# Row slots of 1280 bytes, and the recurrence's 64x64 products laid over four quadrants of the array

## The chip, the cores and the metric

The kernel runs on one core of one Trainium2 chip. A core has TensorE (PE; its weight loads are listed as PEld), VectorE (DVE), ScalarE (ACT), GpSimd (POOL) and SyncE (SP), which issues most of the DMAs. Times are device microseconds (us) of one execution; the time of a kernel is the median of its runs. One execution of each kernel is also profiled, and the rows of the profile come from that one.

## The reference

One inference step of one layer of a hybrid decoder, for a prompt of 256 tokens and 8 single sampled tokens (T = 264 columns in all), width 2048, in fp32:

```python
x = x + 0.5 * swiglu(rmsnorm(x, n1), f1g, f1u, f1d)          # FFN1, 2048 -> 5504 -> 2048
h = rmsnorm(x, nm)
proj = h @ w_in
q, k, v = split(proj)                                        # 16 query heads, 4 kv heads of 64
o_att = sliding_window_attention(q, k, v, sinks)             # window 128
o_rwkv, shift, S = rwkv_time_mix(proj[..., ATT_COLS:], ...)  # 16 heads of 64
x = x + concat(o_att, o_rwkv) @ w_out
x = x + 0.5 * swiglu(rmsnorm(x, n2), f2g, f2u, f2d)          # FFN2
y = rmsnorm(x, final_norm)
```

The core of the time mixing is a recurrence over the tokens, for every head with a state S of 64x64:

```python
sa = einsum('bhij,bhj->bhi', S, -kk_t)
S = S * exp(lw_t)[:, :, None, :] + sa[..., None] * (kk_t * a_t)[:, :, None, :] + v_t[..., None] * k_t[:, :, None, :]
y_t = einsum('bhij,bhj->bhi', S, r_t)
```

## The kernel before

All activations lie transposed: 128 features of a row tile on the partitions, the 264 tokens in the columns. The three big parts are FFN1, the mixing (w_in, attention, recurrence, w_out) and FFN2.

**The big products.** `gemm` streams the weights in chunks of 128x512 (256 KB). SP loads a chunk (`raw`), ACT casts it to the rounded type (`hi`, L132), DVE subtracts to get the rest (`lo`, L59). Activations are split likewise into a hi and a lo row. Each 128x128 weight tile then makes three products of 264 columns, all at L75 (the helper `mm`): hi with the hi row, hi with the lo row, lo with the hi row. There are 14976 such products. In the profile they are `acc<-x,hi` and `acc<-x,lo`, where x, h, o, y or kv is the tile of the activation rows.

**The rows.** `blk` makes one tile of n slots, `ROW` floats apart, of which 264 are used; `pairs` takes the odd slot as a hi row and the even slot before it as its lo row. The rows of h (the hidden layer of an FFN) have slots of the same size in a tile of the FFN's own pool. In FFN2 that pool also holds a small tile `rt`, which stands ahead of h.

```python
t = sp.tile([P, n * ROW + (16 if tag == "y" else 0)], dt, tag=tag, bufs=1, name=uid(tag))
return [t[:, j * ROW:j * ROW + T] for j in range(n)]
```

**Side work in ticks.** After each chunk (twelve products) `gemm` calls `tick`, which moves every running generator on to its next `yield`; `pause(n)` is n ticks. A generator's instructions are so written between the chunks of the big products. A scheduler then fixes the order on each engine, near to this order.

**The recurrence** is done in chunks: 256 tokens are 4 chunks (c) of 64, and 16 heads are 8 pairs (a pair's two heads, h = 0 and 1, on the partitions 0 to 63 and 64 to 127), which go in 4 batches of 2 pairs (k). `prep` runs per pair. It makes the products of keys and queries of each chunk (`gm`), the tiles KR and BT, and near its end two sets of small products: `gv`, with the V rows that lie in `uv` (two quadrants of the array off the diagonal), and `dps`, with the states of the sampled tokens (`XD`, on the diagonal quadrants). `chain` runs per batch, when the pairs are prepared:

- DVE solves a triangular system of 32 rows for each half chunk (tiles `st`, `Xt`, `X`), which ends in TN and TT. Then come `pause(7)`, two small products with a copy after each, and a tick.
- `wus`: TT times two slices of KR at once gives W and U in one product of 64x64 by 128 columns, into one bank for each pair. ACT and DVE copy W (L622) and U (L626, into `uv`). A tick.
- `pbs`: W times BT, and W times gm (the two heads on the two diagonal quadrants); PT is copied from the first, KR takes the second in a sum.
- pN and pY: uv times BT and gm, with all 128 rows.
- three steps of the state, c = 1 to 3, a tick apart: PT times S, then S times KR into pY, then two sums on DVE.
- Ys is copied from pY on ACT; then a group norm on the way to w_out. The last batch also transposes XD (five products, L701) and copies them to XR (L703, L704), which the sampled tokens' state update reads in FFN2.

w_out takes its rows in three passes: the pairs of batches 0 and 1, those of batches 2 and 3, the attention's.

Of the kernel before, what the change touches and what calls it, by code (L numbers as in the profile page):

```python
# [30 lines left out]
ROW = 288  # L31
# [4 lines left out]
PW = (2, 1, 3, 2, 9)  # L36
ALPHA = math.exp(-0.5)
# [10 lines left out]
def body(tc, I, O):  # L48
# [47 lines left out]
    def pause(n):  # L96
        for _ in range(n):
            yield

    with ExitStack() as ctx:  # L100
# [21 lines left out]
        def mp():  # L122
            return pp.tile([P, 512], F32, tag="m", bufs=NM, name=uid("m"))
# [233 lines left out]
        def mixing_body(mx, n2, n3, XD, XR):  # L357
# [68 lines left out]
            def prep(p, bt, k, xrr, xk, xv):  # L426
# [126 lines left out]
            def chain(bt):  # L553
# [35 lines left out]
                yield from pause(7)  # L589
# [20 lines left out]
                yield  # L610
# [3 lines left out]
                wus = [mp() for _ in range(n)]  # L614
                for k in range(n):
                    for c in range(4):
                        for h in range(2):
                            r = HALF[h]
                            mm(wus[k][r, c * P:c * P + P], TT[r, k * 4 + c, :], bt.KR[k][r, 0:3:2, c, :])
                for k in range(n):  # L620
                    v = wus[k].rearrange("p (c t) -> p c t", c=4)
                    (A.copy, V.tensor_copy)[k % 2](W[:, k], v[:, 1:4, 0:64])  # L622
                for k in range(n):
                    v = wus[k].rearrange("p (c t) -> p c t", c=4)
                    for h in range(2):
                        (V.tensor_copy, A.copy)[h](uv[HALF[h], :, k, HALF[h]], v[HALF[h], :, 64:128])  # L626
                yield
                pbs = [mp() for _ in range(n)]
                for k in range(n):
                    for c in range(1, 4):  # L630
                        x = (c - 1) * P
                        for h in range(2):
                            r = HALF[h]
                            mm(pbs[k][r, x:x + 64], W[r, k, c - 1, :], bt.BT[k][r, c, r])
                        for h in range(2):
                            r = HALF[h]
                            mm(pbs[k][r, x + 64:x + P], W[r, k, c - 1, :], bt.Gm[k][h][r, c, 64:128])
                for k in range(n):
                    v = pbs[k][:, :384].rearrange("p (c t) -> p c t", c=3)
                    A.copy(PT[:, k], v[:, :, 0:64])  # L640
                    tt(V, bt.KR[k][:, 1, 1:4, :], v[:, :, 64:128], bt.KR[k][:, 1, 1:4, :], ALU.add)
# [7 lines left out]
                for k in range(n):  # L649
                    for c in range(4):  # L650
                        x = (k * 4 + c) * 64
                        for h in range(2):
                            r = HALF[h]
                            mm(pY[r, x:x + 64], uv[:, c, k, r], bt.Gm[k][h][:, c, 64:128],
                               k + c == 0, c == 0, skip_group_check=True)
# [4 lines left out]
                for c in range(1, 4):  # L660
                    ps = mp()
                    for k in range(n):
                        for h in range(2):
                            r = HALF[h]
                            mm(ps[r, k * 64:k * 64 + 64], PT[r, k, c - 1, :], S[r, k])
                    for k in range(n):
                        for h in range(2):
                            r = HALF[h]
                            x = (k * 4 + c) * 64
                            mm(pY[r, x:x + 64], S[r, k], bt.KR[k][r, 1, c, :], False, True, skip_group_check=True)  # L670
# [26 lines left out]
                if len(bts) == nbat and bt is bts[-1]:  # L697
                    ps = mp()
                    xt = mp()
                    for i in range(5):  # L700
                        TE.transpose((ps, xt)[i > 3][0:64, i % 4 * P:i % 4 * P + P], XD[:, i, :, :], ident)  # L701
                    for h in range(2):
                        A.copy(XR[HALF[h], 0:4], ps[0:64].rearrange("p (c t) -> p c t", c=4)[:, :, HALF[h]])  # L703
                        A.copy(XR[HALF[h], 4], xt[0:64, HALF[h]])  # L704
# [226 lines left out]
            for pi, ks in enumerate(PASS):  # L931
# [24 lines left out]
                k0 += len(ks)  # L956
            n3.to += pairs(blk("o", 8, F32R), *late, *xs4[:2])
            return xr

        def second_ffn(n3, xr, XR):  # L960
# [153 lines left out]
```

## Time and profile before

| | us |
|---|---|
| median of 3 runs (lowest, highest) | 1962.74 (1962.64, 1966.27) |
| the profiled execution | 1962.1 |
| its span | 1960.3 |
| PE busy in the span | 1944.7 (99%) |
| DVE busy | 1314.4 (67%) |
| ACT busy | 1036.9 (53%) |
| POOL busy | 264.0 (13%) |

The granted clock of TensorE was 0.998 in the mean. By stage: FFN1 lies at 0 to 757 us, the mixing with w_out at 757 to 1204, FFN2 after that. In the rows, "acc" is a bank for a big product and "m" a bank for a small one. The rows of the timeline give start, duration, engine, line, operation, output and inputs, shapes and a count. One fp32 product of two 64x64 tiles has two records in it. A matmul's duration runs over several others behind it, since they are pipelined: what one costs is read from start to start.

### The profile page before, as it was taken

Reading aid. Unit: us, or ns where it says so; the run is one execution under the profiler, and the core shown is the slowest. Engines: PE = TensorE matmul, PEld = TensorE weight load, DVE = VectorE, ACT = ScalarE, POOL = GpSimd, SP = SyncE. Lnnn points to the kernel's source line nnn. Section 1 sums busy time; section 2 is a strip of 40 time slices with the busy share of each in tenths; the row PEclk is TensorE's granted clock in tenths of the full one; section 3 lists DMA queues with packets and bytes.
Section 4 is the critical chain, followed back from the end, with each engine's and each line's share of the span. In section 5 each row is a group of like instructions: output and inputs, shape, how many; then the busy total and the mean of one; then the engine's idle time right before and its main releaser. Section 6 shows DMA issues by size and latency. Waiting matters only on the chain.

```text
span 1960.3 us, 45229 instructions
## 1 busy us (share of the span) xinstructions
PE 1944.7 (99%) x17011; PEld 1926.7 (98%) x17011; DVE 1314.4 (67%) x2591; ACT 1036.9 (53%) x2069; POOL 264.0 (13%) x382
## 2 busy tenths in 40 slices
PE   9999999999999999999999999999999999999998
PEld 9999999999999999999989999999999999999998
DVE  5865555655556567799988766866666666666665
ACT  5644444444444456666556755644444444444445
POOL 0401001010010122232210000210101001010012
PEclk9999999999999999999999999999999999999999
DMA  7666666656656567555556455566666666666664
GB/s 241 179 195 193 188 193 194 187 187 179 189 180 187 184 198 226 165 168 147 140 143 176 139 155 183 176 185 187 191 188 196 184 191 190 190 194 183 192 180 148
DMA packets 218875, 357.26 MB, mean 182 GB/s; under 512 B 33552, under 2 KB 72352, under 8 KB 218656
## 3 DMA queue, kind: packets, MB, share of 16 engines
q1 hardware_dynamic: 212144, 345.76, 58.9%
q10 hardware_dynamic: 6512, 8.61, 1.4%
q8 instruction: 133, 2.18, 0.4%
q14 instruction: 86, 0.70, 0.1%
HBM read 346.67 MB, written 9.69 MB: 182 GB/s over the span
## 4 chain that ended last, share of the span: by engine, by line
PE 96%; DVE 2%; issue 1%; DMA 1%; ACT 0%; SPq 0%; DVEq 0%; ACTq 0%
PE acc L75 87%; PE m L75 8%; DVE lo L59 0%; DVE Xt L59 0%; DVE st L59 0%; ACT t L69 0%; DMA x<-in_x 0%; DMA raw<-in_win 0%; DVE y L59 0%; PE m L516 0%; SPq L564 0%; DMA Xt<-sa 0%; PE m L782 0%; PE m L474 0%; DVE t L442 0%
## 5 line engine op out<-in xcount | busy, mean ns | idle before, releaser
L59 DVE TENSOR_TENSOR lo<-raw,hi 128x512 fp32r<-128x512 f32 (+1 forms) x1288 | 875.2, 683 | 513.7 <-ACT hi L132 490.7
L132 ACT CAST hi<-raw 128x512 fp32r<-128x512 f32 (+1 forms) x1288 | 777.6, 607 | 826.0 <-PE acc L75 751.7
L75 PE MATMUL acc<-x,hi 128*128 128x264 f32 x5034 | 932.3, 285 | 1.6 <-DVE o L62 1.3
L75 PEld LDWEIGHTS acc<-x,hi 128*128 128x128 f32 x5034 | 772.4, 188 | 5.2 <-ACT hi L132 1.8
L75 PE MATMUL acc<-x,lo 128*128 128x264 f32 x2517 | 708.0, 282 | 0.4 <-DVE lo L59 0.3
L75 PE MATMUL acc<-h,hi 128*128 128x264 f32 x2752 | 498.1, 284 | 0.0
L75 PEld LDWEIGHTS acc<-x,lo 128*128 128x128 f32 x2517 | 473.0, 188 | 2.6 <-DVE lo L59 1.0
L75 PEld LDWEIGHTS acc<-h,hi 128*128 128x128 f32 x2752 | 420.3, 188 | 0.0
L75 PE MATMUL acc<-h,lo 128*128 128x264 f32 x1376 | 382.6, 280 | 0.0
L75 PEld LDWEIGHTS acc<-h,lo 128*128 128x128 f32 x1376 | 258.0, 188 | 0.0
L59 POOL TENSOR_TENSOR t<-t,t 128x264 f32<-128x264 f32 x74 | 80.0, 1081 | 1099.8 <-DVE t L59 796.1
L75 PE MATMUL acc<-y,hi 128*128 128x264 f32 x648 | 122.9, 284 | 0.0
L75 PE MATMUL acc<-o,hi 128*128 128x264 f32 x648 | 120.5, 283 | 0.0
L75 PE MATMUL acc<-kv,hi 128*128 128x264 f32 x582 | 109.5, 283 | 0.0
L75 PEld LDWEIGHTS acc<-y,hi 128*128 128x128 f32 x648 | 100.3, 188 | 0.1
L75 PEld LDWEIGHTS acc<-o,hi 128*128 128x128 f32 x648 | 99.3, 188 | 0.0
L62 DVE SCALAR_TENSOR_TENSOR x<-acc,x 128x264 f32<-128x264 f32 x192 | 81.1, 427 | 25.1 <-PE acc L75 24.3
L75 PE MATMUL acc<-y,lo 128*128 128x264 f32 x324 | 90.8, 280 | 0.0
L75 PE MATMUL acc<-o,lo 128*128 128x264 f32 x324 | 90.7, 280 | 0.0
L59 DVE TENSOR_TENSOR t<-acc,t 128x264 f32<-128x264 f32 x156 | 67.4, 432 | 32.7 <-PE acc L75 32.7
L75 PEld LDWEIGHTS acc<-kv,hi 128*128 128x128 f32 x582 | 89.2, 188 | 0.0
L75 PE MATMUL acc<-kv,lo 128*128 128x264 f32 x291 | 81.5, 280 | 0.0
(280 smaller groups left out, 1533.9 us busy)
## 6 DMA issues: line engine op xcount, KB each, us to landing
raw<-in_gu SPq DMA_DIRECT2D x688, 256.0 KB, 3.4
raw<-in_dn SPq DMA_DIRECT2D x224, 256.0 KB, 2.8
raw<-in_win SPq DMA_DIRECT2D x152, 256.0 KB, 3.4
raw<-in_dn SPq DMA_DIRECT2D x160, 192.0 KB, 2.7
raw<-in_wout SPq DMA_DIRECT2D x64, 256.0 KB, 3.4
xsp<-x ACTq DMA_DIRECT2D x16, 132.0 KB, 3.1
x<-xsp SPq DMA_DIRECT2D x16, 132.0 KB, 4.1
ld<-in_sT SPq DMA_DIRECT2D x16, 128.0 KB, 3.4
```

The lines of the kernel that those rows point to most:

```text
L59: return e.tensor_tensor(out=out, in0=a, in1=b, op=op)
L62: return V.scalar_tensor_tensor(out=out, in0=a, scalar=s, in1=b, op0=op0, op1=op1)
L75: return TE.matmul(out, lhsT, rhs, start=start, stop=stop, **k)
L132: A.copy(hi[:, :w], raw[:, :w])
```

## The change

- `ROW` goes from 288 to 320 floats: slots of 1280 bytes for every tile of rows. `rt` in FFN2 goes from 16 to 48 floats.
- `gv` and `dps` are written alternately, so that products of diagonal and of off-diagonal quadrants follow each other.
- W and U are separate products of 64x64: U goes to the other half of the partitions (`ub`), W stays (`wb`) and is left out for chunk 0, where nothing reads it. That makes 28 products of 64 columns where 16 of 128 were, in each batch. W is copied by one ACT instruction, U by one on DVE and one on ACT.
- `pbs` becomes `pb` (to the other half) and `gb`, alternating; PT is copied in two ACT instructions.
- In a step of the state, PT times S and S times KR alternate, since pY is now kept with its halves exchanged. Ys is copied back in four pieces, two on ACT and two on DVE.
- `pause(7)` becomes 8 ticks in batch 0; the ticks ahead of W and U, and ahead of `pb`, become two.
- The transposes of XD get a generator of their own (`turned`), three ticks later, with a tick before their copies; what still runs at the end of w_out is drained there.

```diff
-ROW = 288
+ROW = 320
+LAG = (8, 7, 7, 7)
...
-                gv = mp()
-                for c in range(4):
+                gv, dps = mp(), mp()
+                for i in range(NB):
+                    c, g = i // 2, i % 2
                     for h in range(2):
                         r, o = HALF[h], HALF[1 - h]
-                        mm(gv[r, c * 64:c * 64 + 64], bt.Gm[k][h][o, c, 0:64], bt.UV[o, c, k, r])
+                        mm(dps[r, 2 * i:2 * i + 2], st[i // 4][r, i % 4, :], XD[r, 6:8, p, i])
+                        if h == g:
+                            mm(gv[r, c * 64:c * 64 + 64], bt.Gm[k][h][o, c, 0:64], bt.UV[o, c, k, r])
                 A.copy(KR[:, 2], gv[:, :256].rearrange("p (c t) -> p c t", c=4))
-                dps = mp()
-                for i in range(NB):
-                    for h in range(2):
-                        r = HALF[h]
-                        mm(dps[r, 2 * i:2 * i + 2], st[i // 4][r, i % 4, :], XD[r, 6:8, p, i])
...
-                yield from pause(7)
+                yield from pause(LAG[bt.i])
...
-                yield
+                yield from pause(2)
...
-                wus = [mp() for _ in range(n)]
+                ub, wb = mp(), mp()
                 for k in range(n):
                     for c in range(4):
+                        x = (k * 4 + c) * 64
                         for h in range(2):
-                            r = HALF[h]
-                            mm(wus[k][r, c * P:c * P + P], TT[r, k * 4 + c, :], bt.KR[k][r, 0:3:2, c, :])
-                for k in range(n):
-                    v = wus[k].rearrange("p (c t) -> p c t", c=4)
-                    (A.copy, V.tensor_copy)[k % 2](W[:, k], v[:, 1:4, 0:64])
-                for k in range(n):
-                    v = wus[k].rearrange("p (c t) -> p c t", c=4)
-                    for h in range(2):
-                        (V.tensor_copy, A.copy)[h](uv[HALF[h], :, k, HALF[h]], v[HALF[h], :, 64:128])
-                yield
-                pbs = [mp() for _ in range(n)]
+                            r, o = HALF[h], HALF[1 - h]
+                            mm(ub[o, x:x + 64], TT[r, k * 4 + c, :], bt.KR[k][r, 2, c, :])
+                            if c:
+                                mm(wb[r, x:x + 64], TT[r, k * 4 + c, :], bt.KR[k][r, 0, c, :])
+                v = wb[:, :n * 256].rearrange("p (k c t) -> p k c t", k=n, c=4)
+                A.copy(W, v[:, :, 1:4, :])
+                v = ub[:, :n * 256].rearrange("p (k c t) -> p c k t", k=n, c=4)
+                for h in range(2):
+                    (V.tensor_copy, A.copy)[h](uv[HALF[h], :, :, HALF[h]], v[HALF[1 - h]])
+                yield from pause(2)
+                pb, gb = mp(), mp()
                 for k in range(n):
                     for c in range(1, 4):
-                        x = (c - 1) * P
+                        x = (k * 3 + c - 1) * 64
                         for h in range(2):
-                            r = HALF[h]
-                            mm(pbs[k][r, x:x + 64], W[r, k, c - 1, :], bt.BT[k][r, c, r])
-                        for h in range(2):
-                            r = HALF[h]
-                            mm(pbs[k][r, x + 64:x + P], W[r, k, c - 1, :], bt.Gm[k][h][r, c, 64:128])
+                            r, o = HALF[h], HALF[1 - h]
+                            mm(pb[o, x:x + 64], W[r, k, c - 1, :], bt.BT[k][r, c, r])
+                            mm(gb[r, x:x + 64], W[r, k, c - 1, :], bt.Gm[k][h][r, c, 64:128])
...
                         for h in range(2):
-                            r = HALF[h]
+                            r, o = HALF[h], HALF[1 - h]
                             mm(ps[r, k * 64:k * 64 + 64], PT[r, k, c - 1, :], S[r, k])
-                    for k in range(n):
-                        for h in range(2):
-                            r = HALF[h]
-                            x = (k * 4 + c) * 64
-                            mm(pY[r, x:x + 64], S[r, k], bt.KR[k][r, 1, c, :], False, True, skip_group_check=True)
+                            mm(pY[o, x:x + 64], S[r, k], bt.KR[k][r, 1, c, :], False, True, skip_group_check=True)
...
-                    A.copy(Ys[k][:, :NP], pY[:, k * NP:(k + 1) * NP])
+                    for h in range(2):
+                        (A.copy, V.tensor_copy)[h](Ys[k][HALF[h], :NP], pY[HALF[1 - h], k * NP:(k + 1) * NP])
...
-                rt = fp.tile([88, 16], F32, name="rt")
+                rt = fp.tile([88, 48], F32, name="rt")
```

What the change does to the order of PE's instructions is shown at two stretches of batch 1 and one of the preparation. A row has its number, its line, the operation, output and inputs with the tiles' numbers, the shape, and how often it follows itself. `acc` rows are big products, `kr,TT` the W and U products, `BT,W` and `gm,W` those of `pbs` or `pb` and `gb`.

PE before, batch 1, around the W and U products:

```order
5246 L75 MATMUL acc_13959<-x_107,lo_14007 128x264
5247 L75 MATMUL acc_13959<-x_108,hi_14036 128x264 x2
5248 L75 MATMUL acc_13959<-x_108,lo_14037 128x264
5249 L75 MATMUL acc_13959<-x_108,hi_14036 128x264
5250 L75 MATMUL m_13583<-kr_11703,TT_12420 64x128 x8
5251 L75 MATMUL m_13584<-kr_12069,TT_12420 64x128 x8
5252 L75 MATMUL acc_13959<-x_108,hi_14036 128x264
5253 L75 MATMUL acc_13959<-x_108,lo_14037 128x264
5254 L75 MATMUL acc_13959<-x_108,hi_14036 128x264 x2
```

The same place after the change:

```order
5346 L76 MATMUL acc_13963<-x_109,lo_14100 128x264
5347 L76 MATMUL acc_13963<-x_109,hi_14099 128x264 x2
5348 L76 MATMUL m_13625<-kr_11703,TT_12420 64x64
5349 L76 MATMUL m_13626<-kr_11703,TT_12420 64x64
5350 L76 MATMUL m_13625<-kr_11703,TT_12420 64x64 x3
5351 L76 MATMUL m_13626<-kr_11703,TT_12420 64x64
5352 L76 MATMUL m_13625<-kr_11703,TT_12420 64x64
5353 L76 MATMUL m_13626<-kr_11703,TT_12420 64x64
5354 L76 MATMUL m_13625<-kr_11703,TT_12420 64x64
5355 L76 MATMUL m_13626<-kr_11703,TT_12420 64x64
5356 L76 MATMUL m_13625<-kr_11703,TT_12420 64x64
5357 L76 MATMUL m_13626<-kr_11703,TT_12420 64x64
```

Two rows of eight 128-column products are now a run of single 64-column products that alternate between U's bank (the lower number) and W's; the second pair's follow in the same manner.

PE before, batch 1, from the W and U products to the first reader of W:

```order
5251 L75 MATMUL m_13584<-kr_12069,TT_12420 64x128 x8
5252 L75 MATMUL acc_13959<-x_108,hi_14036 128x264
5253 L75 MATMUL acc_13959<-x_108,lo_14037 128x264
5254 L75 MATMUL acc_13959<-x_108,hi_14036 128x264 x2
5255 L75 MATMUL acc_13959<-x_108,lo_14037 128x264
5256 L75 MATMUL acc_13959<-x_108,hi_14036 128x264 x2
5257 L75 MATMUL acc_13959<-x_108,lo_14037 128x264
5258 L75 MATMUL acc_13959<-x_109,hi_14077 128x264 x2
5259 L75 MATMUL acc_13959<-x_109,lo_14078 128x264
5260 L75 MATMUL acc_13959<-x_109,hi_14077 128x264
5261 L75 MATMUL m_13638<-BT_12288,W_13184 64x64 x2
5262 L75 MATMUL m_13638<-gm_12206,W_13184 64x64
```

After the change, the last of the large products ahead of that reader, and the reader:

```order
5380 L76 MATMUL acc_14138<-x_106,hi_14140 128x264 x2
5381 L76 MATMUL acc_14138<-x_106,lo_14141 128x264
5382 L76 MATMUL acc_14138<-x_107,hi_14194 128x264 x2
5383 L76 MATMUL acc_14138<-x_107,lo_14195 128x264
5384 L76 MATMUL acc_14138<-x_107,hi_14194 128x264 x2
5385 L76 MATMUL acc_14138<-x_107,lo_14195 128x264
5386 L76 MATMUL acc_14138<-x_107,hi_14194 128x264 x2
5387 L76 MATMUL acc_14138<-x_107,lo_14195 128x264
5388 L76 MATMUL m_13714<-BT_12288,W_13195 64x64
5389 L76 MATMUL m_13715<-gm_12206,W_13195 64x64
5390 L76 MATMUL m_13714<-BT_12288,W_13195 64x64
5391 L76 MATMUL m_13715<-gm_12242,W_13195 64x64
```

Before, 12 large products stand between the last W product and the first product that reads W; after the change 22 do (with two transposes of a pair being prepared among them), and BT,W and gm,W alternate one by one, where two of the one and two of the other went together.

PE before, preparation of a pair, `gv` (uv,gm) and `dps` (XD):

```order
5170 L75 MATMUL m_13367<-uv_11876,gm_13247 64x64
5171 L75 MATMUL m_13367<-uv_11876,gm_13283 64x64
5172 L75 MATMUL m_13367<-uv_11876,gm_13247 64x64
5173 L75 MATMUL m_13367<-uv_11876,gm_13283 64x64
5174 L75 MATMUL m_13367<-uv_11876,gm_13247 64x64
5175 L75 MATMUL m_13367<-uv_11876,gm_13283 64x64
5176 L75 MATMUL m_13367<-uv_11876,gm_13247 64x64
5177 L75 MATMUL m_13367<-uv_11876,gm_13283 64x64
5178 L75 MATMUL m_13377<-XD,ld_13287 64x2 x8
5179 L75 MATMUL m_13377<-XD,ld_13289 64x2 x8
```

After the change, the same pair:

```order
5253 L76 MATMUL m_13379<-XD,ld_13298 64x2
5254 L76 MATMUL m_13378<-uv_11876,gm_13258 64x64
5255 L76 MATMUL m_13379<-XD,ld_13298 64x2 x3
5256 L76 MATMUL m_13378<-uv_11876,gm_13294 64x64
5257 L76 MATMUL m_13379<-XD,ld_13298 64x2
5258 L76 MATMUL m_13378<-uv_11876,gm_13258 64x64
5259 L76 MATMUL m_13379<-XD,ld_13298 64x2 x3
5260 L76 MATMUL m_13378<-uv_11876,gm_13294 64x64
```

The eight uv,gm products stood ahead of the sixteen XD products; each now stands between XD products.

More of the change, by code (lines that the diff above doesn't have):

```diff
@@ L638, in chain @@
+                            mm(gb[r, x:x + 64], W[r, k, c - 1, :], bt.Gm[k][h][r, c, 64:128])
+                v = pb[:, :n * 192].rearrange("p (k c t) -> p k c t", k=n, c=3)
+                for h in range(2):
+                    A.copy(PT[HALF[h]], v[HALF[1 - h]])
+                v = gb[:, :n * 192].rearrange("p (k c t) -> p k c t", k=n, c=3)
                 for k in range(n):
-                    v = pbs[k][:, :384].rearrange("p (c t) -> p c t", c=3)
-                    A.copy(PT[:, k], v[:, :, 0:64])
@@ L678, in chain @@
                 for k in range(n):
-                    A.copy(Ys[k][:, :NP], pY[:, k * NP:(k + 1) * NP])
+                    for h in range(2):
+                        (A.copy, V.tensor_copy)[h](Ys[k][HALF[h], :NP], pY[HALF[1 - h], k * NP:(k + 1) * NP])
                     A.copy(Ys[k][:, NP:T], XD[:, 7, bt.p0 + k, :])
@@ L697, in chain, with turned @@
                 if len(bts) == nbat and bt is bts[-1]:
[L698 to L704, printed above, removed]
+                    spawn(turned())
+                yield
+            def turned():
+                yield from pause(3)
+                ps, xt = mp(), mp()
+                for i in range(5):
+                    TE.transpose((ps, xt)[i > 3][0:64, i % 4 * P:i % 4 * P + P], XD[:, i, :, :], ident)
+                yield
+                for h in range(2):
+                    A.copy(XR[HALF[h], 0:4], ps[0:64].rearrange("p (c t) -> p c t", c=4)[:, :, HALF[h]])
+                    A.copy(XR[HALF[h], 4], xt[0:64, HALF[h]])
                 yield
@@ L956, in mixing_body @@
                 k0 += len(ks)
+            drain(list(tasks))
             n3.to += pairs(blk("o", 8, F32R), *late, *xs4[:2])
```

6 lines of the change are left out of this document (3 added, 3 removed).

## Prediction

> **What bounds the kernel now.** I read the page's busy shares and its chain first, then the busy times cut by stage, then the chain in order of time, and last single rows of the PE timeline.
>
> ```profile
> span 1960.3 us, 45229 instructions
> PE 1944.7 (99%) x17011; PEld 1926.7 (98%) x17011; DVE 1314.4 (67%) x2591; ACT 1036.9 (53%) x2069; POOL 264.0 (13%) x382
> PE 96%; DVE 2%; issue 1%; DMA 1%; ACT 0%; SPq 0%; DVEq 0%; ACTq 0%
> ```
> ```profile
> 0.00:66.00 66.00, 64.84 (x509) 63.93 (x510) 45.62 (x78) 38.99 (x75) 8.26 (x18) 1.00 0.67 218
> 66.00:757.00 691.00, 691.00 (x5760) 691.00 (x5760) 419.49 (x711) 344.46 (x619) 89.90 (x89) 1.00 0.63 190
> 757.00:1204.00 447.00, 441.11 (x4559) 424.64 (x4559) 361.31 (x962) 278.23 (x700) 73.94 (x177) 1.00 0.55 160
> 1204.00:1960.30 756.30, 747.70 (x6190) 747.09 (x6188) 488.02 (x842) 375.18 (x677) 91.89 (x98) 0.99 0.62 185
> ```
> ```profile
> 65.86 691.26 PE acc L75 x5760
> ...
> 1149.08 54.83 PE acc L75 x457
> ...
> 1258.34 690.05 PE acc L75 x5712
> ```
>
> The second block has, after start and end, the busy us of PE, PEld, DVE, ACT and POOL, the granted clock, the DMA share and GB/s. TensorE carries 96% of the chain, at full clock. In FFN1 (66 to 757) it never pauses: 691.26 / 5760 = 120.01 ns for each 264-column product. So only three things can move the end: how long one large product takes, how long the small products of the recurrence hold TensorE in the mixing stage (757 to 1204), and the waits there, at most 447.0 - 441.1 = 5.9 us of idle time. ACT and DVE copies count only where they make TensorE wait.
>
> **Row slots.** A slot was 288 floats, 1152 bytes, which is four and a half times 256; now it is 1280, five times 256. Before, the hi and lo rows of a pair (neighbouring slots) start half a 256-byte line apart; afterwards all start alike. The `rt` tile grows by 32 floats (128 bytes), which shifts the rows of h in FFN2 by the same half line. Does placement change a product's time? FFN1 and FFN2 run the same code on the same shapes, and their h rows differ in placement: in FFN2 the hi and lo rows have swapped half lines. The time by tile h (FFN2 first, then FFN1):
>
> ```profile
> 1290.00:1948.00 658.00, 251.39 (x2063) 1.00 0.62 186
> 66.00:757.00 691.00, 248.70 (x2064) 1.00 0.63 190
> ```
>
> Equal counts and equal clock, 2.69 us apart. The long piece of FFN2 in the chain says the same of all its products: 690.05 / 5712 = 120.81 ns, 0.80 above FFN1's; x 5712 that is 4.6 us. The w_out piece has 54.83 / 457 = 119.98, nothing to win. I take it that rows placed alike run at FFN1's 120.0, and credit 4.6, rounded to **-5 us** for some loss inside the mixing stage that no long piece shows. No row has the new placement (hi and lo alike), so the ends are the two tile rows: 120.5 (248.70 / 2064, which holds the overlap at the ends of stretches) against 121.9 (251.39 / 2063), 1.36 ns apart. All 14976 large products going the bad way would be +20 us; the good end is -6. I take the good end, since most of the program's rows are at it already.
>
> **Four quadrants.** A 64x64 product in fp32 appears as two records (16 products kr,TT as x32). Rows of batch 3's chain, and of batch 1's preparation:
>
> ```profile
> 1065.09 1.96 PE L75 MATMUL m<-kr,TT 64*64 64x128 f32 x32
> 1066.98 0.33 PE L782 MATMUL m<-C,t 128*128 128x128 f32 x1
> ...
> 1070.27 0.28 PE L75 MATMUL m<-BT,W 64*64 64x64 f32 x4
> 1070.39 0.28 PE L75 MATMUL m<-gm,W 64*64 64x64 f32 x4
> 1070.50 0.28 PE L75 MATMUL m<-BT,W 64*64 64x64 f32 x4
> ...
> 1071.79 1.28 PE L75 MATMUL m<-uv,BT 128*64 128x64 f32 x31
> 1072.85 0.22 PE L75 MATMUL m<-gm,uv 128*64 128x64 f32 x1
> ```
> ```profile
> 1079.31 0.45 PE L75 MATMUL m<-S,PT 64*64 64x64 f32 x8
> 1079.59 0.40 PE L75 MATMUL m<-kr,S 64*64 64x64 f32 x8
> 1079.92 0.28 PE L75 MATMUL m<-qb,ld 128*128 128x8 f32 x1
> ```
> ```profile
> 940.11 0.51 PE L75 MATMUL m<-uv,gm 64*64 64x64 f32 x10
> 940.40 0.22 PE L75 MATMUL m<-XD,ld 64*64 64x2 f32 x2
> 940.45 0.23 PE L75 MATMUL m<-uv,gm 64*64 64x64 f32 x2
> 940.48 0.20 PE L75 MATMUL m<-XD,ld 64*64 64x2 f32 x2
> 940.50 0.22 PE L75 MATMUL m<-uv,gm 64*64 64x64 f32 x2
> 940.54 0.20 PE L75 MATMUL m<-XD,ld 64*64 64x2 f32 x2
> 940.56 0.23 PE L75 MATMUL m<-uv,gm 64*64 64x64 f32 x2
> 940.60 0.73 PE L75 MATMUL m<-XD,ld 64*64 64x2 f32 x20
> ...
> 942.45 0.49 PE L75 MATMUL m<-tw,ld 65*128 65x264 f32 x1
> ```
>
> With two quadrants in use, eight records (four BT, four gm) start in 0.23 us: 29 ns each. At 940.11 gm alone has 10 in 0.29, the same. Between 940.40 and 940.60 the gm products (off-diagonal quadrants) and the XD products (diagonal) go together, and 12 records start in 0.20 us: 17 ns each. Four quadrants nearly double the rate; I price an alternated record at 14.5 (half of 29) to 17.
> - W and U (kr,TT): 16 products of 128 columns take 1.89 us. They become 28 of 64 columns, 56 records: 24 products in fours, 48 x 14.5 to 17 = 0.70 to 0.82, and four U products of chunk 0 in pairs, 8 x 29 = 0.23, with about 0.1 to change over: 1.03 to 1.15. Saving 0.74 to 0.86, in four batches 3.0 to 3.4.
> - BT,W and gm,W: 48 records, 1.39 at 29, become 0.70 to 0.82: 0.57 to 0.69, in four batches 2.3 to 2.8.
> - A step of the state (S,PT and kr,S): 0.61 us for 16 records, of which 16 x 29 = 0.46 is rate. 0.23 to 0.27 afterwards: 0.19 to 0.23 for each of 12 steps, 2.3 to 2.8.
> - gv with XD: 2.34 us for two pairs (32 gm records, 64 XD). XD alone runs at 0.53 / 20 = 26 ns, so 64 are 1.7, with gm under them: 1.8 with the change-over, at most 0.5 saved, less since part of it overlaps already: 1.2 to 2.0 over four.
>
> Sum 8.8 to 11; I take **-10 us**. All of it lies on the path, as TensorE is busy there.
>
> The Trainium skill ("TensorE: Matmul & The Clock Gate", Part 3, The mechanism) says that a weight load overlaps products in flight only when its row group differs. In the new order W and U of one head share rows, so by that rule nothing doubles, and this part of the sum is about 0. The trace does not bear it out: uv,BT uses all 128 rows in every product and only changes column halves, and starts at (1072.85 - 1071.79) / 31 = 34 ns, near the 29 of products that differ in rows.
>
> **Waits.** A tick is a chunk of twelve large products, 12 x 120.0 = 1.44 us. The first and second dependent steps get one tick more (batch 0 also one ahead of them), and the five transposes of XD move to a task of their own, three ticks later.
>
> ```profile
> PE m L75 <- DVE W L622: 1.4, 2, 1.1
> ...
> PE m L75 <- DVE PT L59: 1.0, 1, 1.0
> PE m L75 <- ACT TT L609: 0.7, 1, 0.7
> PE m L701 <- ACT XR L703: 0.4, 1, 0.4
> ```
> ```profile
> 1022.84 0.35 DVE L622 COPY W<-m 128x192 f32<-128x192 f32 x1
> ```
>
> In batches 1 and 2 TensorE waits for W's second copy, which stands on DVE behind the solve of a later batch; it is one ACT copy now, and by the new order 22 large products lie between W's products and their use where 12 lay: 1.2 us more, and the longest of the two waits is 1.1. I take 1.4 off. The XR wait goes too (0.4; `XR` is next read in FFN2). The waits for TN (PT, 1.0) and TT (0.7) stay: the orders show batch 0's products after TN in the same place of the stream, and as many as before behind TT in batch 1. **-2 us**; ends 0 (each moves elsewhere) and -4 (TT and the smaller ones go as well). What is late next is uv: its DVE half is now one of 64x512, behind the same solve, but uv is read behind BT,W, 0.8 us on. Each batch ends two ticks later; that is covered by the large products of the next batch, and in the last batch by w_out, whose first pass needs batches 0 and 1 only. The two Ys copies that move to DVE replace a W and a uv copy there: 0.
>
> **What takes some back.** A large product also needs its lo chunk, which DVE subtracts, and in places DVE has nothing to spare:
>
> ```profile
> 840.00:860.00 20.00, 20.00 (x163) 19.70 (x162) 19.64 (x55) 13.47 (x32) 7.43 (x14) 1.00 0.57 175
> 980.00:1000.00 20.00, 18.67 (x148) 18.15 (x148) 19.95 (x44) 12.68 (x26) 4.50 (x11) 1.00 0.52 147
> ```
>
> DVE is at 19.6 and 19.95 of 20 us, and around 990 PE idles 1.3 us. Where DVE is full, a shorter TensorE only waits longer. If a fifth of the stage is like that, a fifth of 12 us returns: **+2.5**, from 0 to +8.
>
> **Sum.** -5 - 10 - 2 + 2.5 = -14.5 on the profiled 1962.1 us (span 1960.3 and 1.8 around it): 1947.6. The median of the three runs, 1962.74, lies 0.6 above it: **1948 us**, own range 1941 to 1955. A measurement here tells about 0.2%, 4 us, from no change.
>
> **Rivals.**
> - DVE sets the pace in most of mixing, or the waits move instead of going: row slots -5, quadrants and waits -12, +11 back, about 1957; its half above 1959 is no change. For it: the two full rows. Against: DVE is busy 361 of the stage's 447 us.
> - Products that share rows don't overlap: 56 records at 29 are 1.6 us against 1.89, the rest as before; slots and waits stay: about 1955.
> - Slower: rows placed alike run like FFN2's h. At 1.36 ns on all 14976 it is +20, with -9.5 for the rest: about 1973. It decides from about 0.65 ns a product on. For it: no row shows the new placement. Against: hi and lo start unlike in both rows that differ, so neither is a sign of it.
> - Rows placed alike are faster than any seen: 1 ns is 15 us, 3 ns would give about 1905. No row speaks for it but that placement counts.
>
> **Chances.** Forecast 0.60, DVE or moved waits 0.17, no overlap 0.09, slower placement 0.09, faster placement 0.05. Faster by over 0.2%: 0.60 + 0.09 + half of 0.17 + 0.05 = 0.82; within: 0.09; slower: 0.09. The range 1937 to 1961 leaves out the two placement rivals and the tail.
>
> **What would show it.** FFN2's h time at 248.7 and its long piece at 120.0 ns a product (slots); W and U rows alternating, in 1.0 to 1.2 us a batch, and BT,gm in 0.8 (quadrants); no wait of PE for W or XR (waits); DVE near 20 of 20 with PE waiting for lo, or a new wait for uv, would be the first rival. A long piece of FFN1 off 120.0 would make the whole forecast wrong.

## The result and the profile after

Over twelve runs each, the changed kernel takes 1962.63 us (1959.22 to 1964.30) and the kernel before 1966.44 us (1962.64 to 1967.94): a ratio of 0.9984 with a 95% interval of 0.9977 to 0.9992. That is some 3 us, where 14.5 were forecast, and 1.6 us outside the range. The profiled executions are 1962.1 us before and 1962.95 us after. They do not show the gain, because the profiled run of before was a quick one: its granted clock was 0.998, and it lies 4.3 us under the median of the twelve.

The page of the changed kernel, and its mixing stage among the busy times by stage (PE, PEld, DVE, ACT, POOL, clock, DMA share, GB/s):

```profile
span 1961.2 us, 45431 instructions
PE 1937.3 (99%) x17107; PEld 1919.6 (98%) x17107; DVE 1317.8 (67%) x2591; ACT 1039.8 (53%) x2067; POOL 258.7 (13%) x382
PE 96%; DVE 2%; ACT 1%; issue 1%; DMA 0%; DVEq 0%; ACTq 0%
```
```profile
757.00:1204.00 447.00, 433.64 (x4608) 417.27 (x4607) 362.17 (x955) 278.88 (x692) 69.25 (x177) 0.98 0.55 158
```

TensorE is busy 7.5 us less in the stage's window (433.64 for 441.11), with DVE at its 362. Two columns are new: PE now idles 447.0 - 433.6 = 13.4 us there, where it was 5.9, and the granted clock is 0.98 where it was 1.00. The chain in order of time shows what the two stages make of it:

```profile
65.74 691.23 PE acc L76 x5760
...
1150.25 59.09 PE acc L76 x492
...
1263.77 685.48 PE acc L76 x5712
```

FFN1 is as before. FFN2's long piece takes 685.48 us for its 5712 products, 120.0 ns each, where it took 690.05: 4.6 us won. But it starts at 1263.77 where it started at 1258.34: **the mixing stage is 5.4 us longer**. The gain of the rows was paid back by the recurrence.

The quadrants themselves do what was forecast. In batch 2 the 56 records of W and U take 1.21 us to the next product's start, by the PE timeline:

```profile
1018.57 1.28 PE L76 MATMUL m<-kr,TT 64*64 64x64 f32 x56
1019.78 0.27 PE L734 MATMUL m<-C,dkv 128*8 128x128 f32 x1
```

Before, they took 1.89 us there. In the other three batches they now take 1.08 to 1.09, where they took 1.89 to 2.27. Counted in this way, to the start of the next product and without waits or half clock, all four parts of the quadrants can be read from the two traces. W and U saved 3.5 us over the batches, BT,W and gm,W 3.2, the twelve steps of the state 12 x (0.61 - 0.39) = 2.6, and gv with XD 1.0: together 10.3.

What took the time is in PE's waits:

```profile
PE m L76 <- DVE Xt L60: 3.4, 1, 3.4
PE acc L76 <- DVE o L63: 3.1, 1, 3.1
PE m L76 <- ACT uv L626: 1.6, 2, 1.4
```

The first is in batch 2, and DVE's timeline tells why: U's copy to uv stands behind the solve of batch 3 (st, Xt) and starts 7 us after the W and U products are done. PE has finished BT,W and gm,W long before:

```profile
1026.92 0.23 DVE L60 TENSOR_TENSOR st<-X,Xt 128x70 f32<-128x70 f32 x1
1027.18 0.69 DVE L626 COPY uv<-m 64x512 f32<-64x512 f32 x1
1027.79 0.22 DVE L60 TENSOR_TENSOR Xt<-Xt,st 128x70 f32<-128x70 f32 x1
```
```profile
1024.40 0.22 PE L76 MATMUL m<-gm,W 64*64 64x64 f32 x1
1028.02 0.30 PE L76 MATMUL m<-uv,BT 128*64 128x64 f32 x2 [3.40 <-DVE Xt L60]
```

The second long wait is near 992 us, for the attention's `o` on a full DVE. Cut into pieces of 2 us (PE busy, clock, DMA share, GB/s), it shows the other cost:

```profile
990.00:992.00 2.00, 1.08 (x9) 1.00 0.65 193
992.00:994.00 2.00, 0.00 (x0) 1.00 0.19 69
994.00:996.00 2.00, 1.86 (x10) 0.65 0.58 155
996.00:998.00 2.00, 2.00 (x11) 0.50 0.37 108
998.00:1000.00 2.00, 2.00 (x18) 1.00 0.36 82
```

PE stands still for over 3 us, and then **runs at half clock** for some 3.4: 10 or 11 products in 2 us instead of 17. There are four stretches at half clock in the stage, from 994, 1011, 1028 and 1080 us. The first three last 3.4 us each, the fourth 6.8; half of these 17.1 us, 8.5 us, is lost. The run shown of the kernel before has none in this stage. Only the first and the third stand behind a wait of over 3 us. Ahead of the second there is no wait over 0.5 us, but 3.8 us of small products; ahead of the fourth stand a wait of 0.94 us and products of 8 columns. So 5.1 of the 8.5 us are not explained by long waits.

The account of the mixing stage: 7.5 us more idle time and 8.5 us of lost clock, less what the quadrants saved, give the +5.4 that was measured. By this the quadrants saved 10.6 us, in agreement with the 10.3 read from their own rows and with the size forecast.

### The profile page after: what moved, and what is told of

Same layout as the page of the kernel before. It is cut to its first block, busy times and chain, and to the rows that moved or that the text cites. A ratio compares the mean times of both kernels' runs of the same rounds, so it can differ in the third digit from the quotient of the medians.

```text
span 1961.2 us, 45431 instructions
## 1 busy us (share of the span) xinstructions
PE 1937.3 (99%) x17107; PEld 1919.6 (98%) x17107; DVE 1317.8 (67%) x2591; ACT 1039.8 (53%) x2067; POOL 258.7 (13%) x382
## 4 chain that ended last, share of the span: by engine, by line
PE 96%; DVE 2%; ACT 1%; issue 1%; DMA 0%; DVEq 0%; ACTq 0%
PE acc L76 88%; PE m L76 7%; DVE lo L60 1%; ACT t L70 0%; DVE y L60 0%; DMA x<-in_x 0%; DVE st L60 0%; DVE Xt L60 0%; ACT hi L133 0%; DVE t L777 0%; ACT BT L522 0%; ACT L70 0%; PE m L517 0%; DMA ld<-in_sT 0%; DVE uv L626 0%
## 5 line engine op out<-in xcount | busy, mean ns | idle before, releaser
L76 PEld LDWEIGHTS acc<-x,hi 128*128 128x128 f32 x5034 | 785.4, 190 | 6.9 <-DVE o L63 3.4
L76 PE MATMUL acc<-x,lo 128*128 128x264 f32 x2517 | 721.2, 287 | 0.8 <-DVE lo L60 0.8
L76 PE MATMUL acc<-h,lo 128*128 128x264 f32 x1376 | 387.8, 284 | 0.0
```

The source lines that it names most:

```text
L76: return TE.matmul(out, lhsT, rhs, start=start, stop=stop, **k)
```

## The experiments

My theory after the result: the rows win 4.6 us; the quadrants win about 10 on TensorE; but there TensorE is at the pace of VectorE's in-order queue, so the time turns into waits, and waits over some length halve the clock behind them. The rivals: a half clock that comes from using four quadrants, not from idling; waits that only the one copy of U causes; or the added ticks as the cause. Ratios are to the kernel before on the same chip, with 95% intervals; not all kernels of a section ran on one chip.

### The rows: alone, left out, and with the old rt

```diff
-ROW = 288
+ROW = 320
...
-                rt = fp.tile([88, 16], F32, name="rt")
+                rt = fp.tile([88, 48], F32, name="rt")
```

The first kernel is the old one with these lines alone, the second the changed one without them, the third the old one with `ROW` alone.

> The kernel before, with the slots of 320 floats and the larger rt tile alone. If the row slots do what the two traces show in FFN2 (690.05 us for 5712 products before, 685.48 after), this is 4.6 us faster than before, a ratio of 0.9977, and FFN2's long piece is again at 120.0 ns a product. If the slots only moved something else in the whole change, its ratio is 1.000 and the long piece stays at 120.8.

> The changed kernel with the old slots (288 floats, rt of 16). If the slots are worth 4.6 us and the rest of the change gains about 10 on TensorE and gives it all back in the mixing stage (7.5 us of new idle time and 7.8 us of half clock), this is as fast as before within 2 us, a ratio of 0.999 to 1.001. If the rest of the change has a gain of its own that the slots spoil, it is faster than the changed kernel, under 0.997.

> The kernel before with slots of 320 floats and the old rt: in FFN2 the rows of h start half a 256-byte line away from all other rows, but hi and lo alike. If it matters that a pair's hi and lo start alike, FFN2's h products are at 120.0 ns as with the larger rt. If it matters where they start, h's products stay near the 121.9 ns of before, and FFN2's long piece is at about 686.9 to 688 us in place of 685.5.

Measured: rows alone 0.9978 (0.9968 to 0.9988); the changed kernel with old rows 1.0014 (1.0005 to 1.0023), a little above what was expected; of the third kernel, one run. FFN2's long piece with rows alone, and the third kernel's piece and h rows (FFN1, FFN2):

```profile
1259.01 685.49 PE acc L75 x5712
```
```profile
1258.82 687.65 PE acc L75 x5712
```
```profile
66.00:757.00 691.00, 248.66 (x2064) 1.00 0.64 190
1290.00:1948.00 658.00, 250.65 (x2064) 1.00 0.63 186
```

So the rows are worth what was forecast, and all of the change's gain is theirs; with the old rows, the rest of the change makes the kernel slower by 0.0014. The third kernel splits the gain: slots of 1280 bytes alone give 2.4 us of 4.6 (687.65), the shift by `rt` the other 2.2. There hi and lo of h start alike and h in FFN2 still takes 250.65 us, not 248.66 as in FFN1: where the rows start counts, not only that a pair starts alike. Only starts 128 bytes apart were compared; that placement repeats every 256 bytes, as the prediction's reasoning has it, no run shows.

### The wait for U, and idle time on purpose

The changed kernel with both copies of U on ScalarE:

```diff
-                    (V.tensor_copy, A.copy)[h](uv[HALF[h], :, :, HALF[h]], v[HALF[1 - h]])
+                    A.copy(uv[HALF[h], :, :, HALF[h]], v[HALF[1 - h]])
```

> The changed kernel with both copies of U on ScalarE, so that neither stands behind the solve on VectorE. The 3.4 us wait of batch 2 goes. If the clock's half rate behind it (1028 to 1032 us) comes from that idle time, it goes too, and the kernel is about 5 us faster than the changed one, a ratio of 0.996 to before. If the half rate has nothing to do with the wait (for instance comes from the use of four quadrants), the granted clock there stays at 0.5 and it is 3.4 us, 0.9967. If the wait only moves to the next reader, it is the changed kernel's 0.998.

Measured: 0.9987 (0.9979 to 0.9996), no gain. The wait for U is gone, and its time stands elsewhere:

```profile
PE m L76 <- DVE Xt L60: 5.0, 2, 3.0
PE acc L76 <- DVE o L63: 3.3, 1, 3.3
PE m L76 <- ACT TT L608: 2.4, 1, 2.4
```

The rows on Xt are now waits of N,PT, the next reader, behind the same solve. The wait moved, as the third of the cases expected. A new wait of 2.4 us for TT, with TensorE almost wholly idle from 1020 to 1022 us, has no half clock behind it (pieces of 2 us: PE busy, clock, DMA share, GB/s):

```profile
1020.00:1022.00 2.00, 0.02 (x2) 1.00 0.31 86
1022.00:1024.00 2.00, 1.94 (x61) 1.00 0.44 115
```

Next, waits in the kernel before, far from any small products:

```diff
...
+        def gap(k):
+            ps, pt, g = mp(), mp(), tmp()
+            for j in range(2):
+                behind(mm(ps[:, j * P:j * P + P], ones, ones))
+            A.copy(g[:, :256], ps[:, :256])
+            for _ in range(k):
+                tt(G, g[:, :256], g[:, :256], g[:, :256], ALU.add)
+            held[0] = mm(pt[:, :P], ones, g[:, :P])
...
+                    if begin and pi and o == 8:
+                        gap(pi)
```

> The kernel before, with five added waits of TensorE in FFN1, one in each of its later parts: a small product waits for a copy on ScalarE and 1, 2, 3, 4 and 5 additions on GpSimd, about 1 us each, and the next large product stands behind it. No four quadrants are used there. If idle time lowers the granted clock, the long ones (3 us and over) are followed by some 3.4 us at 0.5, which cost 1.7 us each beside the gap, and the short ones are not. If idle time is not the cause, the clock stays at 1.00 behind all five, and the time is longer by the gaps alone, about 20 us.

One run: 1992.49 us. Two of the five gaps, and the pieces of 2 us behind them (PE busy, clock, DMA share, GB/s):

```profile
248.84 0.49 PE L76 MATMUL m<-t,ones 128*128 128x128 f32 x2 [1.15 <-POOL t L60]
```
```profile
373.95 0.49 PE L76 MATMUL m<-t,ones 128*128 128x128 f32 x2 [1.84 <-POOL t L60]
```
```profile
248.00:250.00 2.00, 1.16 (x9) 1.00 0.74 214
250.00:252.00 2.00, 2.00 (x19) 1.00 0.11 35
...
374.00:376.00 2.00, 2.00 (x12) 0.71 0.28 97
376.00:378.00 2.00, 2.00 (x11) 0.50 0.00 0
378.00:380.00 2.00, 2.00 (x17) 0.94 0.47 128
```

After 1.15 us of idling the clock stays at 1.00; after 1.84 us (2.1 from start to start of the products) it falls to 0.5, and so after the three longer ones. The pieces behind the second gap lack 2 x (0.29 + 0.50 + 0.06) = 1.7 us of full clock, half of 3.4 us. So idle time alone is enough, and the rival that it takes four quadrants falls: FFN1 has no such products. The Trainium skill ("TensorE: Matmul & The Clock Gate", HAM oscillation) describes this, with gaps over some 3.4 us as the limit. The trace does not agree with the limit, as 1.84 us of idling were enough here.

The length of the gap alone does not decide, however: the 2.4 us in the kernel above were harmless. Nor does it take a gap: in this same run, with the old products, the clock falls at 1112 us (0.56 and 0.50 in the next two pieces of 1 us), and TensorE was busy all through the 3.4 us before, 1.8 us of them with products of 8 columns. Within a trace, all slow stretches start a whole number of times 3.41 us apart: in the changed kernel at 994.6, 1011.7, 1028.7 and 1079.9 us, which is 5, 5 and 15 times. That would fit a clock that is set at fixed moments by what TensorE did since the last one; this was not tested. Whether the quadrants have a part in the two stretches of the changed kernel without a long wait stays open too.

The last kernel of this section fills the wait for U with 24 idle products in batch 2:

```diff
+                for _ in range(24 if bt.i == 2 else 0):
+                    mm(pN[:, :P], ones, ones)
```

> The changed kernel with 24 products of ones (128x128, their result not used) ahead of batch 2's uv,BT, where TensorE waits 3.4 us for U. They add work and take nothing away. If idle time lowers the clock, TensorE has no gap there now, the stretch behind (1028 to 1032 us) stays at 1.00 in place of 0.5, and the kernel is 1 to 2 us faster in spite of the added work, 0.997 to 0.998. If not, the clock is 0.5 there all the same, and the time is the changed kernel's or up to 1 us more.

```profile
1024.90 5.62 PE L76 MATMUL m<-ones 128*128 128x128 f32 x48
1030.45 1.15 PE L76 MATMUL m<-uv,BT 128*64 128x64 f32 x32
```
```profile
1028.00:1030.00 2.00, 2.00 (x20) 1.00 0.14 46
1030.00:1032.00 2.00, 2.00 (x57) 1.00 0.27 67
```

The clock stays at 1.00 where it was 0.5, as expected, but the kernel is slower: 1.0017 (1.0008 to 1.0026). The 48 records took 5.5 us and so outlasted the wait by 2; and N,PT then waited 3.3 us for DVE, with half clock behind that wait instead.

### Ticks alone, quadrants alone

The first is the changed kernel with the old ticks (below; the last edit stands at both places), the second the old products with new rows and new ticks (and the moved transposes):

```diff
-LAG = (8, 7, 7, 7)
+LAG = (7, 7, 7, 7)
...
-                yield from pause(2)
+                yield
```

> The changed kernel with the ticks as before (7 for every batch, one tick ahead of W and U and ahead of pb); quadrants, rows and the moved transposes stay. If the longer spacing is what pushes the solve of one batch onto the next one's copies, the 3.4 us wait for U and the 3.3 us wait for o shrink, the clock stays up, and it is 5 to 10 us faster than the changed kernel, 0.993 to 0.996 of before. If the spacing does what it is written for, W's and PT's products wait for their copies instead, and it is as fast as the changed kernel or slower, 0.998 or more.

> The kernel before with the new rows and the new ticks (and the moved transposes), but the old products on two quadrants. Beside the kernel with the rows alone (0.9978) this tells what the ticks cost by themselves. If the ticks cause the new waits, they are here too, with half clock behind them, and it is 5 us or more slower than rows alone, 1.000 and over. If TensorE's shorter work is what uncovers VectorE, there are no waits over 2 us here and the ratio stays at 0.997 to 0.998.

Measured: quadrants without ticks 0.9981 (0.9972 to 0.9990), ticks without quadrants 0.9999 (0.9990 to 1.0007). With rows alone at 0.9978 and both at 0.9984, the ticks (with the moved transposes) cost 4 us with the old products, and with the new ones nothing that the intervals tell; the quadrants gain nothing without the ticks. With the old products the ticks bring a wait of 3.0 us for `lo` on VectorE and a slow stretch behind it, so they make waits of their own. The mixing stage of the kernel without ticks, where its FFN2 starts, and its one slow stretch there:

```profile
757.00:1204.00 447.00, 433.23 (x4649) 416.22 (x4648) 363.34 (x961) 281.96 (x697) 72.69 (x177) 1.00 0.56 160
```
```profile
1259.24 685.48 PE acc L76 x5712
```
```profile
1084.00:1086.00 2.00, 2.00 (x18) 0.92 0.64 157
1086.00:1088.00 2.00, 2.00 (x23) 0.50 0.77 254
1088.00:1090.00 2.00, 2.00 (x14) 0.73 0.35 71
```

This is the cleanest sight of the loss. PE is busy 7.8 us less than with rows alone (441.0), and FFN2 starts at 1259.24 where rows alone start it at 1259.01. The stage's clock rounds to 1.00; the slow stretch costs 1.7 us. So of some 9 us that the quadrants saved, 7.8 have become idle time and 1.7 lost clock. Of the 13.8 us that PE idles in the stage, 10.6 are waits for VectorE.

### VectorE with less to do

If VectorE's queue sets the pace, the quadrants must pay once it has room. Three kernels have the recurrence's sixteen reciprocals replaced by a quick operation:

```diff
-                V.reciprocal(b, nps[:, :T])
+                ts(V, b, nps[:, :T], 0.0, ALU.mult, 2.8e-5, ALU.add)
...
-                V.reciprocal(r, r)
+                ts(V, r, r, 0.0, ALU.mult, 0.1, ALU.add)
```

> The kernel before with the new rows alone, and with VectorE relieved: the sixteen reciprocals of the recurrence's heads (1.80 us each) are replaced by a multiply-and-add of about 0.43 us that writes a constant, so the normalisation of the keys and of the group norm is left out. That takes some 22 us off VectorE in the mixing. If TensorE is bound by its own work there, it gains little, 2 to 4 us of the 5.4 us of waits, so a ratio of 0.996 to 0.997. If VectorE sets the pace, more.

> The changed kernel with the same sixteen reciprocals left out. If VectorE hides the gain of the quadrants, then with VectorE relieved the waits of 13.4 us fall below 6, the clock stays at 0.997 or more, and it is 6 to 10 us faster than the kernel with rows alone and the same relief: a ratio of 0.990 to 0.993. If the quadrants gain nothing on TensorE's side, or the order of dependent steps makes the waits whatever VectorE has to do, it stays at the same ratio as its partner or above it.

> The changed kernel with the old ticks and the same sixteen reciprocals left out. Beside the two others this tells ticks from quadrants once VectorE has room: if the ticks are what spreads the steps far enough, it has 3 us or more of waits for W, U and PT and is slower than the changed kernel with the same relief; if they only delay, it is as fast or faster, 0.990 to 0.993.

Measured: rows alone 0.9974 (0.9963 to 0.9984), the changed kernel 0.9940 (0.9927 to 0.9954), the one without ticks 0.9944 (0.9931 to 0.9956). Rows alone hardly move (0.9978 before); with the quadrants the same relief brings 0.0044, less than was expected. The two now differ by 0.0034, 6.7 us, where they could not be told apart. The chain's FFN2 piece, rows alone and changed:

```profile
1260.45 685.48 PE acc L75 x5712
```
```profile
1254.85 685.48 PE acc L76 x5712
```

The changed one still has one wait of 6.4 us (`kr,TT` for TT's copy on ACT), so this is not yet all of the 10 us. **The gain is there, and VectorE's part of the recurrence hides it.** Ticks or none make no difference that can be told.

Can it be had with nothing left out? Three more ways were tried. One chunk's lo part in four to GpSimd, in the changed kernel:

```diff
...
-                hi, lo = ready or chunk(src[:, k0 * P:k1 * P], k1 - k0, V, ahead)
+                hi, lo = ready or chunk(src[:, k0 * P:k1 * P], k1 - k0, G if k0 == ease else V, ahead)
...
-                gemm(ps, I["win"][t], n2.xs, tick)
+                gemm(ps, I["win"][t], n2.xs, tick, ease=12)
```

> The changed kernel with the lo part of every fourth chunk of w_in subtracted on GpSimd instead of VectorE (38 of 152, some 26 us of VectorE's 362 in the mixing). If VectorE's load there is what makes TensorE wait, the idle time of 13.4 us falls below 8, the clock stays nearer to 1.00, and the kernel is 6 to 10 us faster than the changed one, 0.993 to 0.995. If the order of the dependent steps makes the waits whatever VectorE's load, it stays at 0.998; a slower GpSimd that holds up the lo chunks would show as waits for lo on POOL and a ratio above 0.998.

Slower, 1.0040 (1.0027 to 1.0053). VectorE's busy time over the span is 1319.3 us where the changed kernel has 1317.8, though some 26 us were taken off it: other operations of VectorE became longer. Of the costliest groups in the mixing, one in the changed kernel and the same with the lo parts on GpSimd:

```profile
L63 DVE SCALAR_TENSOR_TENSOR t<-pj,nmu,t 128x264 f32<-128x264 f32 x24 | 11.5, 485 | 1.2 <-ACT t L70 1.0
```
```profile
L63 DVE SCALAR_TENSOR_TENSOR t<-pj,nmu,t 128x264 f32<-128x264 f32 x24 | 15.9, 662 | 5.9 <-ACT t L70 5.7 <-ACT t L415 0.2
```

The sixteen reciprocals to GpSimd, for the same three kernels:

```diff
...
-                V.reciprocal(b, nps[:, :T])
+                A.copy(b, nps[:, :T])
+                tt(G, b, b, bc(neg, (P, T)), ALU.pow)
...
-                V.reciprocal(r, r)
+                tt(G, r, r, bc(neg, (P, T)), ALU.pow)
```

> The kernel before with the new rows, and the recurrence's sixteen reciprocals computed on GpSimd (as a power of -1, with a copy on ScalarE ahead of the eight that read a bank) instead of VectorE. Nothing is left out. If GpSimd does one in 2 us or less, this is the kernel with rows alone or a little faster, 0.997 to 0.998; if one takes many microseconds there, its steps come later and the kernel is slower than 1.000.

> The changed kernel with the same sixteen reciprocals on GpSimd. If VectorE's load is what hides the quadrants' gain, and GpSimd is quick enough, this is 4 to 8 us faster than its partner with rows alone, 0.993 to 0.995, and faster than both kernels. If the gain only showed because the normalisations were left out, it stays at 0.998.

> The changed kernel with the old ticks and the sixteen reciprocals on GpSimd. As fast as the one with the new ticks, 0.993 to 0.995, if ticks no longer matter once VectorE has room; faster than it if the added ticks only delay.

Ratios of 1.2616, 1.2735 and 1.2621: one power takes 42.5 us, which answers nothing about the quadrants. The costliest group of GpSimd in the first of them:

```profile
L59 POOL TENSOR_TENSOR t<-t,neg 128x264 f32<-128x264 f32 x16 | 679.9, 42499 | 44.9 <-ACT t L69 34.7 <-ACT t L444 10.1
```

Last, plain copies to ScalarE, for the same three; the edit of the second is shown, and the first moves the W and U copies of the old products instead:

```diff
-                    (V.tensor_copy, A.copy)[h](uv[HALF[h], :, :, HALF[h]], v[HALF[1 - h]])
+                    A.copy(uv[HALF[h], :, :, HALF[h]], v[HALF[1 - h]])
...
-                        (A.copy, V.tensor_copy)[h](Ys[k][HALF[h], :NP], pY[HALF[1 - h], k * NP:(k + 1) * NP])
+                        A.copy(Ys[k][HALF[h], :NP], pY[HALF[1 - h], k * NP:(k + 1) * NP])
...
-                    V.tensor_copy(s0, tp[:, 256:384])
+                    A.copy(s0, tp[:, 256:384])
```

> The kernel before with the new rows, and VectorE relieved by copies alone: W, U and the third of an attention tile's transposes (0.29 to 0.41 us each, 28 copies, some 9 us) go to ScalarE. Nothing is left out. With the old products TensorE has little idle time to win back: 0.996 to 0.998.

> The changed kernel with U, Ys and the same transposes' copies on ScalarE (some 10 us off VectorE, under half of what leaving out the reciprocals took). If VectorE's load hides the quadrants' gain, some of it shows: 3 to 5 us faster than the changed kernel, 0.9955 to 0.997, and as fast as its partner with rows alone or faster. If only the order of dependent steps counts, it stays at 0.998 or more, and ScalarE's queue takes VectorE's place among the waits.

> The changed kernel with the old ticks and the same copies on ScalarE. 0.9955 to 0.997 likewise if VectorE's load is what counts; if it is faster than the one with the new ticks by 2 us or more, the ticks only delay.

Measured: 1.0006 (0.9998 to 1.0015), 0.9999 (0.9990 to 1.0007) and 0.9995 (0.9986 to 1.0004): the first clearly slower than without the edit, the others no faster. VectorE is busy 10 us less in the second's stage, and TensorE idles 15.3 us there, where it idled 13.4. The waits of the second:

```profile
PE m L76 <- DVE st L60: 6.9, 2, 4.7
PE acc L76 <- DVE o L63: 3.3, 1, 3.3
```

So VectorE's busy time alone is not the measure. What the reciprocals have and the copies have not is length: 1.8 us, in a queue that runs in order. Leaving them out takes off load and also shortens the steps that the solve waits for; which of the two counts was not told apart. No kernel that computes everything beat the one with the rows alone, and that one (0.9978) is not told from the changed kernel (0.9984).

## Why the prediction was wrong, step by step

- **Row slots, -5: right.** 4.57 us in FFN2's long piece, 0.9978 for the rows alone. Its reason was half right: the third kernel of the first group has hi and lo alike and only 2.4 of the 4.6 us.
- **Four quadrants, -10: right on TensorE, wrong for the time.** The rate was sized rightly (W and U in 1.08 to 1.21 us, forecast 1.03 to 1.15; 10.3 us in all). "All of it lies on the path, as TensorE is busy there" is the sentence that failed. TensorE was 98.7% busy in that stage, but its work came at the pace at which VectorE handed it over, and a shorter TensorE waited longer.
- **Waits, -2: wrong in sign.** W's wait went from 1.4 to 0.2 us and XR's is gone, as said. But the idle time grew by 7.5 us. I named uv as what is late next and put no price on it: "0.8 us on" was set against a copy that came 7 us after its products.
- **"Each batch ends two ticks later; that is covered": wrong** with the old products, where the ticks, with the moved transposes, cost 4 us (0.9999 against 0.9978).
- **What takes some back, +2.5 (0 to +8): mis-sized**, by taking a fifth of the stage as bound by VectorE. Without ticks, 7.8 us came back as idle time; in the changed kernel it was 7.5, and 8.5 more of lost clock.
- **The clock was not in the sum at all.** Nothing in the profile of before showed it: its longest gap of TensorE in the mixing was 1.6 us, and the run shown had no slow stretch there. One cannot read the price of a 3 us gap from a trace that has none.
- **The base.** The sum was made on the profiled 1962.1 us, 4.3 us under the median of the twelve runs. From 1962.1 the measured ratio gives 1959, inside the range; from 1966.44 it gives 1963.3, near the 1962.63 measured.

The first rival (VectorE sets the pace, or the waits move instead of going, about 1957, chance 0.17) is what happened, in its mechanism; its time lacked the clock too. Its evidence against, "DVE is busy 361 of the stage's 447 us", was the mean of a stage that has 840 to 1040 us at 90% in it. The rival that products sharing rows don't overlap (the rule of the Trainium skill, "TensorE: Matmul & The Clock Gate", Part 3, The mechanism) fell: W and U of one head share rows, and 56 records took 1.08 to 1.21 us, some 20 ns each, where its price of 29 made 1.6 us.

## What to carry to other kernels

When one engine is 99% busy and hands work back and forth with another that runs in order, shortening its small steps pays only if the other engine's next result is already there; look at the moment, not at the stage's mean, and try the price first by leaving work out on the other engine. An idle gap of TensorE of some 2 us and more can cost 1.7 us beside its length, as those of 1.84 us and longer in FFN1 did; the harmless 2.4 us show that it need not. Work that only streams, such as the big products here, is where a small gain per product (0.8 ns of 120, from the start of a row) reaches the end in full.

## What the hardware showed that was not expected

- The time of a 264-column product depends on where its moving rows start: h in FFN2 took 251.39, 250.65 and 248.66 us for 2064 products in three placements (before, slots alone, slots and rt).
- 1.84 us of idling in FFN1 halved TensorE's clock for 3.4 us and 1.15 us did not; yet 2.4 us in the recurrence did not either, and a stretch of small products did so without any gap. Slow stretches start a whole number of times 3.41 us apart.
- A power on GpSimd takes 42.5 us for 128x264, a VectorE reciprocal 1.80.
- Some of VectorE's operations with two inputs became longer while GpSimd subtracted: 662 ns for 485.
